# The place of the queries' part in the second half's list of projections

## The chip, the cores and the metric

One core of a Trainium2 chip runs the whole step. The metric is the device time of one execution in microseconds (us). The engines are named as in the profile: PE is the matrix engine (PEld its weight loads), DVE the vector engine, ACT the scalar engine, POOL the GpSimd engine, and SP is the engine whose queue issues nearly all DMAs.

## The reference

One layer is applied to 2048 new frames of a prompt and to 64 frames of a running stream. One projection of the normalised input feeds ten column groups: queries, keys, values and a gate of a differential attention (`qa, ka, va, za`), the same four of a retention branch (`qb, kb, vb, zb`), and two merge gates (`ga, gb`).

```python
h = rmsnorm(x, norm_g) @ w_in
qa, ka, va, za, qb, kb, vb, zb, ga, gb = jnp.split(h, _split_points(), axis=-1)
qa = rmsnorm(qa.reshape(B, T, H_A, 2, DK_A), qn_g)
ka = rmsnorm(ka.reshape(B, T, H_A, 2, DK_A), kn_g)
...
s = jnp.einsum('bqhcd,bkhcd->bhcqk', q, k).astype(jnp.float32) * (DK_A ** -0.5)
s = s - slopes[None, :, None, None, None] * dist[None, None, None]
s = jnp.where(allowed[None, None, None], s, -jnp.inf)
p = jax.nn.softmax(s, axis=-1)
a = p[:, :, 0] - lam * p[:, :, 1]
...
m = ga * (oa @ w_oa) + gb * (ob @ w_ob)
return x + m @ w_out
```

The attention is causal in chunks of 64 frames, so the frames 0 to 1023 need keys and values of the first half alone, and the frames 1024 to 2047 need those of both halves. Everything is float32: every operand of a matrix product is split into a high and a low part of a reduced format, and a product is three matmuls (high by high, high by low, low by high).

## The kernel before, in words

**A planner writes the order out.** The kernel is a set of Python generators, each with a priority. A loop (L197) always advances the most urgent one that may go on by the planner's own clock; a generator yields a time or a condition. The instructions of PE, ACT and DVE stay in the order in which they are written. The clock is an estimate: `P` (L258) adds what a matmul costs on PE, `A`, `V` and `G` what ACT, DVE and POOL take. `take` and `give` (L214, L255) hand out numbered buffers of SBUF and banks of PSUM with the time from which they are free.

**Two streams share PE.** `w_stream` (L2961) makes the projections. Its priority is the lowest (9), so that it fills PE wherever nothing else may run. `z_stream` (L3064, priority 4) makes the attention: first the running stream's, then for each half of the prompt four heads of four pairs of row blocks (`attn_head`, L1845), where `qk_block` makes the scores (L1878, L1879), `softmax` works on ACT and DVE, and `at_pv` transposes (L1990) and multiplies by the values (L1968 to L1970). The attention of a half waits until `w_stream` has set a mark (`kqv00` and `kqv10`, then `kqv01` and `kqv11`): `h_loader`, `q_loader` and `z_stream` look for it, and `head_in` (L1823) adds 9000 ns of the planner's clock. Retention (`ret_stream`, L2436) is a third, more urgent stream; its second part waits for the mark `ret1`.

**The list of the second half.** In L2996 the projections of frames 1024 to 2047 stand as a list. There are two kinds ahead of the last entry:

- A natural part (`natural`, L1230; in the list `wide[0]` values, `wide[1]` keys, `wide[2]` queries, and `later`, the retention's values) makes 512 columns for eight tiles of 128 frames: 192 matmuls, with the frames' tile held and the weights streaming 512 wide. Its weights come as eight pieces of 128 x 512; all eight are kept for all eight tiles, high and low, so 16 buffers are in use. They are given back one piece after the other during the eighth tile.
- A transposed unit (`transposed`, L1426; `plain[0]` to `plain[10]`) makes 256 columns: 144 matmuls in six groups (the first unit has eight groups and 192). Its weights are four pieces, 8 buffers. `plain[2]` and `plain[3]` are the retention's keys.

The last entry, `quad` (L1544), makes the remaining five column pairs in a form with seven products in place of eight; its x-operands come from DRAM through `x_pass` (L1510).

`m0` and `m1` in the list are the marks `kqv0` and `kqv1`; `(None, "nat")` lets `x_again` and `more_rows` go on.

**Weights.** `w_load` (L661) loads the pieces in the order of `self.order`, which is made from the same list (L2998), into three staging buffers `ws`. `next_piece` (L711) takes two buffers, 12 of the kind `w` and 4 of the kind `wx`; ACT writes the high part (L727), POOL the low part (L748).

**After a projection.** A natural tile of queries goes through `fin_qk` (L1289): ACT squares and copies it, DVE sums and scales, PE transposes it (L1340), ACT and DVE split it, and SP stores it to `qT`. A transposed group is copied by ACT (`fin_t`, L1450) and stored.

**The end.** When the attention and the retention are done, `out_prep` (L2561) loads and splits the weights and operands of the output projections; when `quad` is done too, `out_stream` (L2935) follows.

Of the kernel before, what the change touches and what calls it, by code (L numbers as in the profile page):

```python
# [172 lines left out]
class Hybrid:  # L173
# [2787 lines left out]
    def w_stream(self):  # L2961
# [3 lines left out]
        m0, m1 = (None, "kqv0"), (None, "kqv1")  # L2965
# [7 lines left out]
        wide = [(va, lambda half: self.natural(half, self.fin_va(0, 4), False, True), True),  # L2973
                (ka, lambda half: self.natural(half, self.fin_qk("k", 0, 4), False, True), True),
                (qa, lambda half: self.natural(half, self.fin_qk("q", 0, 4), False, True), True)]
        first = [wva, wk, wq, m0, m1]
        seq = []
        early = [(vb, lambda half: self.natural(half, self.fin_vb(), False, True, True), True)]
# [10 lines left out]
        for base, dst, n in ((za, self.zaT, 2), (zb, self.zbT, 2), (ga, self.gaT, 4), (gb, self.gbT, 4)):  # L2989
            for g in range(n):  # L2990
# [2 lines left out]
        later = [(vb, lambda half: self.natural(half, self.fin_vb(), False, True), True)]  # L2993
        plain = [(c0, lambda half, a=a: self.transposed(*a), False) for c0, a in again[:PLAIN]]
        c0s, args = zip(*again[PLAIN:])
        seqs = [first + early + seq, [plain[0], plain[1], wide[0], wide[1], plain[2], wide[2], m0, m1, plain[3],  # L2996
                                      *later, (None, "nat"), (None, "ret"), *plain[4:],
                                      (c0s, lambda half: self.quad(args), "quad")]]  # L2998
        self.order = [[(c[0], c[2] if len(c) > 2 else False) for c in q if c[0] is not None] for q in seqs]
# [203 lines left out]
```

## Time and profile before

| what | value |
|---|---|
| median of 3 runs (lowest to highest) | 1892.78 us (1887.71 to 1893.15) |
| profiled execution, its own time | 1890.56 us |
| span of its trace, first to last instruction | 1888.8 us |
| PE / DVE / ACT / POOL busy | 1869.9 / 1328.1 / 975.9 / 673.6 us |
| second half's projections in the trace | 585.4 to 1531 us |

A row of the table of stretches gives, for a stretch of the span, its length, each engine's busy time in it with the number of its instructions, the clock that PE was granted (1.00 is full), the share of the DMA engines and their rate. A row of the timeline is start, length, engine, line, operation, output and input. A row of the list of waits names the waiting instruction, the one it waited for, the total, the number of times and the longest. Matmuls overlap: one of 512 columns shows about 0.39 us, and the next one starts some 0.23 us after it.

### The profile page before, as it was taken

What the parts mean: (1) busy time and instruction counts of PE and PEld (TensorE: products, weight loads), DVE (VectorE), ACT (ScalarE), POOL (GpSimd) and SP (SyncE); (2) the same over time, 40 slices, a digit from 0 to 9 for tenths busy, and PEclk for the clock granted to TensorE, in tenths of its full rate; (3) what the DMA queues carried; (4) which work ended last, traced back from release to release, by engine and by line L of the source; (5) the groups of instructions that cost most, each with busy time, mean ns of one, the idle gap of its engine ahead of it and who ended that gap; (6) DMA issues with size and microseconds to landing.
All of it is one profiled execution on the core that took longest, in us unless ns stands there. A gap on an engine that the chain in (4) does not pass through costs nothing.

```text
span 1888.8 us, 33022 instructions
## 1 busy us (share of the span) xinstructions
PE 1869.9 (99%) x11090; PEld 1647.0 (87%) x11090; DVE 1328.1 (70%) x3110; ACT 975.9 (52%) x2266; POOL 673.6 (36%) x730
## 2 busy tenths in 40 slices
PE   9999999999999999999999999999999999999999
PEld 7788888888888888899888899999999999998887
DVE  6765757657584776877477676668787868987664
ACT  6434544555434566555455565556676546654221
POOL 2420356555562203031311345342133545522442
PEclk9999999999999999999999999999999999999999
DMA  8664555666857866564622855854633998986452
GB/s 259 210 178 123 167 155 182 180 197 195 248 181 199 216 195 213 154 198 110 177 73 80 206 147 152 211 141 127 184 110 117 270 248 265 272 255 210 166 157 78
DMA packets 402557, 340.09 MB, mean 180 GB/s; under 512 B 85330, under 2 KB 348626, under 8 KB 401363
## 3 DMA queue, kind: packets, MB, share of 16 engines
q1 hardware_dynamic: 402386, 337.97, 61.4%
q8 instruction: 88, 1.44, 0.3%
q14 instruction: 83, 0.67, 0.1%
HBM read 218.27 MB, written 118.75 MB: 178 GB/s over the span
## 4 chain that ended last, share of the span: by engine, by line
PE 84%; DMA 6%; DVE 5%; issue 1%; POOL 1%; ACT 1%; SPq 1%; DVEq 0%; POOLq 0%; ACTq 0%
PE mm L1137 29%; PE mm L989 8%; PE tp L989 4%; PE at L1990 3%; PE s L1878 2%; PE s L1879 2%; PE s L989 2%; PE pv L1970 2%; PE pv L1969 2%; PE pv L1968 2%; PE mm L1564 2%; PE s L2793 1%; PE s L2795 1%; PE s L2794 1%; PE pv L2256 1%
## 5 line engine op out<-in xcount | busy, mean ns | idle before, releaser
L748 POOL TENSOR_TENSOR wl<-ws,wh 128x512 fp32r<-128x512 f32 x109 | 151.7, 1403 | 232.8 <-ACT wh L727 232.1
L1137 PE MATMUL mm<-wh,xh 128*128 128x512 f32 x504 | 203.5, 404 | 0.0
L1137 PE MATMUL mm<-wl,xh 128*128 128x512 f32 x504 | 198.1, 393 | 1.7 <-POOL wl L748 1.7
L1137 PE MATMUL mm<-wh,xl 128*128 128x512 f32 x504 | 198.3, 393 | 0.0
L1137 PE MATMUL mm<-xh,wh 128*128 128x288 f32 (+2 forms) x544 | 179.1, 329 | 0.0
L1137 PE MATMUL mm<-xl,wh 128*128 128x288 f32 (+2 forms) x544 | 176.0, 323 | 0.0
L1137 PE MATMUL mm<-xh,wl 128*128 128x288 f32 (+2 forms) x544 | 175.9, 323 | 0.0
L1918 ACT ACTIVATE row<-row,a_mx 128x1024 f32<-128x1024 f32 (+7 forms) x144 | 149.9, 1043 | 10.2 <-DVE a_mx L1897 10.0
L2006 DVE TENSOR_TENSOR atl<-at,ath 128x512 fp32r<-128x512 f32 (+1 forms) x144 | 92.9, 658 | 82.6 <-ACT ath L2004 82.1
L2004 ACT CAST ath<-at 128x512 fp32r<-128x512 f32 (+1 forms) x144 | 79.2, 564 | 108.9 <-PE at L1990 106.1
L1745 POOL TENSOR_TENSOR r_y<-r_y,r_sq 128x256 f32<-128x256 f32 x32 | 28.7, 896 | 282.1 <-DVE r_sq L1742 220.5
L856 POOL TENSOR_TENSOR wl<-ws,wh 128x256 fp32r<-128x256 f32 x64 | 54.3, 848 | 197.2 <-ACT wh L847 196.9
L1887 DVE CUSTOM_DVE_ANT_0 row<-s,dfar 128x512 f32<-128x512 f32 (+2 forms) x145 | 89.5, 630 | 38.1 <-PE s L1879 37.7
L1137 PEld LDWEIGHTS mm<-wh,xl 128*128 128x128 f32 x504 | 94.7, 188 | 21.5
L1137 PEld LDWEIGHTS mm<-wl,xh 128*128 128x128 f32 x504 | 95.1, 189 | 19.7 <-POOL wl L748 2.5
L1137 PEld LDWEIGHTS mm<-wh,xh 128*128 128x128 f32 x504 | 94.9, 188 | 17.4 <-DVE raw L1308 0.2
L1137 PEld LDWEIGHTS mm<-xh,wl 128*128 128x128 f32 x544 | 102.6, 189 | 6.7
L1137 PEld LDWEIGHTS mm<-xh,wh 128*128 128x128 f32 x544 | 102.6, 189 | 6.5
L1137 PEld LDWEIGHTS mm<-xl,wh 128*128 128x128 f32 x544 | 102.7, 189 | 6.3
L1940 DVE SCALAR_TENSOR_TENSOR row<-row,a_w 128x1024 f32<-128x1024 f32 (+5 forms) x88 | 98.4, 1123 | 0.0
L1878 PE MATMUL s<-K,q 128*128 128x512 f32 (+3 forms) x238 | 91.1, 385 | 0.6 <-DVE a_acc L1887 0.5
L727 ACT CAST wh<-ws 128x512 fp32r<-128x512 f32 x111 | 67.5, 619 | 45.8 <-DMA ws<-wsum 11.2
(543 smaller groups left out, 6070.0 us busy)
## 6 DMA issues: line engine op xcount, KB each, us to landing
ws<-in_w_in_dram SPq DMA_DIRECT2D x155, 256.0 KB, 3.4
q<-qT SPq DMA_DIRECT2D x128, 128.0 KB, 3.4
K<-kT SPq DMA_DIRECT2D x48, 256.0 KB, 4.7
V<-vN SPq DMA_DIRECT2D x24, 512.0 KB, 6.3
row<-in_x_prompt_dram SPq DMA_DIRECT2D x16, 512.0 KB, 4.5
wz<-in_w_in_dram SPq DMA_DIRECT2D x32, 256.0 KB, 4.4
row<-in_cache_k_T_dram SPq DMA_DIRECT2D x32, 256.0 KB, 3.1
row<-in_cache_v_diff_dram SPq DMA_DIRECT2D x32, 256.0 KB, 3.6
```

The costliest lines, as they stand in the source:

```text
L727: self.nc.scalar.copy(h, st)
L748: eng.tensor_sub(l, st, h.bitcast(F32))
L856: nc.gpsimd.tensor_sub(l[:, cs], src, h[:, cs].bitcast(F32))
L989: nc.tensor.matmul(ps, w[:, c], xs[x][c], start=bool(tag) and c == 0 and i == 0, stop=c == 3 and i == 2, skip_group_check=True)
L1137: nc.tensor.matmul(ps, p, q, start=c == 0 and i == 0, stop=c == KC - 1 and i == 2)
L1878: nc.tensor.matmul(ps, q1s, kk, start=True, stop=False)
L1887: nc.vector.tensor_tensor_reduce(out=row[:, k0:k0 + n], in0=ps, in1=tab, scale=-SLOPES[h], scalar=3.0e38, op0=ALU.add, op1=ALU.min, accum_ ...
L1918: nc.scalar.activation(u, u, AF.Exp, bias=mx, scale=-1.0, accum_out=lp[:, k:k + 1])
L1940: nc.vector.scalar_tensor_tensor(out=u0, in0=u1, scalar=w[:, 0:1], in1=u0, op0=ALU.mult, op1=ALU.add)
L1990: nc.tensor.transpose(at[:, w:w + 128], src, self.ident)
L2004: nc.scalar.copy(ah[:, :w], at[:, :w])
L2006: nc.vector.tensor_sub(al[:, :w], at[:, :w], ah[:, :w].bitcast(F32))
```

## The change

In the list of the second half, `wide[2]` (the queries) and `plain[2]` (the first of the two units of retention keys) change places; the two marks stay right behind the queries and so go ahead of `plain[2]` too. No instruction's form changes, and none is added or left out. The order in which the weight pieces are loaded follows, as it is made from the same list.

```diff
         c0s, args = zip(*again[PLAIN:])
-        seqs = [first + early + seq, [plain[0], plain[1], wide[0], wide[1], plain[2], wide[2], m0, m1, plain[3],
+        seqs = [first + early + seq, [plain[0], plain[1], wide[0], wide[1], wide[2], m0, m1, plain[2], plain[3],
                                       *later, (None, "nat"), (None, "ret"), *plain[4:],
                                       (c0s, lambda half: self.quad(args), "quad")]]
```

## The prediction

> **What bounds the kernel now.** I read the page first, then the table of stretches, then PE's list of waits, then single rows of the timelines of PE and POOL.
>
> ```profile
> span 1888.8 us, 33022 instructions
> ...
> PE 1869.9 (99%) x11090; PEld 1647.0 (87%) x11090; DVE 1328.1 (70%) x3110; ACT 975.9 (52%) x2266; POOL 673.6 (36%) x730
> ...
> PE 84%; DMA 6%; DVE 5%; issue 1%; POOL 1%; ACT 1%; SPq 1%; DVEq 0%; POOLq 0%; ACTq 0%
> ```
>
> PE is idle for 1888.8 - 1869.9 = 18.9 us in all, and the chain that ended last runs through it for 84%. A change of order leaves PE the same matmuls; it can win only what PE idles or loses in clock, and it can lose by making PE idle. So the place of the change comes next, cut where the pieces of the list begin and end (all engines, then the projections of line 1137 alone):
>
> ```profile
> core 0: us, PE busy (x) PEld busy (x) DVE busy (x) ACT busy (x) POOL busy (x), PEclk, DMA share, GB/s
> ...
> 738.30:821.40 83.10, 81.44 (x485) 70.58 (x485) 67.65 (x196) 48.93 (x127) 21.07 (x18) 1.00 0.65 187
> 821.40:859.80 38.40, 38.40 (x269) 35.94 (x268) 26.80 (x80) 21.26 (x53) 6.75 (x7) 1.00 0.60 177
> 859.80:922.60 62.80, 62.80 (x348) 53.80 (x347) 41.45 (x107) 34.21 (x82) 11.21 (x10) 1.00 0.49 134
> 922.60:947.30 24.70, 24.70 (x153) 22.61 (x153) 5.11 (x9) 8.67 (x17) 12.86 (x18) 1.00 0.57 170
> 947.30:1037.40 90.10, 89.84 (x496) 77.16 (x495) 69.35 (x202) 48.96 (x98) 11.11 (x8) 1.00 0.25 75
> 1037.40:1388.50 351.10, 350.53 (x2366) 322.84 (x2365) 255.30 (x723) 204.22 (x454) 122.79 (x197) 1.00 0.61 161
> 1388.50:1460.00 71.50, 70.35 (x551) 68.62 (x548) 60.15 (x132) 49.06 (x103) 23.04 (x16) 1.00 0.41 126
> 1460.00:1531.00 71.00, 68.31 (x536) 67.33 (x535) 54.99 (x90) 33.91 (x59) 40.26 (x28) 1.00 0.92 261
> ```
>
> ```profile
> core 0: us, PE busy (x), PEclk, DMA share, GB/s
> ...
> 821.40:859.80 38.40, 26.54 (x144) 1.00 0.60 177
> 859.80:922.60 62.80, 47.16 (x194) 1.00 0.49 134
> 922.60:947.30 24.70, 24.32 (x145) 1.00 0.57 170
> 947.30:1037.40 90.10, 50.26 (x195) 1.00 0.25 75
> ```
>
> The keys run to 821.4, `plain[2]` (144 matmuls) to 859.8, the queries (192) to 922.6, `plain[3]` (144) to 947.3, the retention's values to 1037.4, the seven other transposed units to 1388.5, `quad` to 1531. The reader should see that PE has no idle time from 821.4 to 947.3, although there is next to no attention in the last of these stretches: `plain[3]` is alone there, at 24.3 us.
>
> ```profile
> 873.48 0.39 PE L1879 MATMUL s<-K,q 128*128 128x512 f32 x1
> ...
> 922.65 0.40 PE L1137 MATMUL mm<-xh,wh 128*128 128x512 f32 x1
> ...
> 950.76 0.39 PE L1878 MATMUL s<-K,q 128*128 128x512 f32 x1
> ```
>
> The first half's last scores are at 873.5. The queries end and the mark is set at 922.65. The second half's first scores are at 950.76, 28.1 us behind the mark.
>
> ```profile
> engine line waited for: us in total, times, longest us
> PE at L1564 <- DVE ev L1584: 1.8, 1, 1.8
> PE mm L1137 <- POOL wl L748: 1.7, 2, 1.0
> ...
> PE tp L1719 <- DVE u L1584: 1.1, 1, 1.1
> PE mm L1564 <- DVE ev L1584: 0.8, 2, 0.5
> ```
>
> These are nearly all of PE's waits between 821 and 1531, but for the POOL line, which lies in the stretch before (83.10 - 81.44 = 1.66 us); I need it below.
>
> **The change part by part.**
>
> *The marks come earlier.* Ahead of them PE has one transposed unit less. Alone that is 24.3 us (the row of `plain[3]`), so the mark moves from 922.65 to about 898.3, and the first scores with the same 28.1 us to about 926.4; `plain[2]` then fills the gap as `plain[3]` does now. This saves nothing by itself: PE is full on both sides, and the 24.3 us of `plain[3]` go among the second half's attention, whose stretches (947.3 to 1388.5) are full too, with 0.26 + 0.57 = 0.83 us idle. Worth 0. If that cover failed, up to 24.3 us would lie open; no row suggests it, as `plain[2]` stands ready.
>
> *Queries directly behind keys.* Both are natural parts, and each holds all 16 buffers. Now a unit with 8 buffers lies between them, and the boundaries at 821.4 and 859.8 cost PE nothing. The nearest row is values to keys, the same kind of neighbours:
>
> ```profile
> 731.31 2.54 POOL L748 TENSOR_TENSOR wl<-ws,wh 128x512 fp32r<-128x512 f32 x2 [7.63 <-ACT wh L727]
> ...
> 748.86 1.26 POOL L748 TENSOR_TENSOR wl<-ws,wh 128x512 fp32r<-128x512 f32 x1
> ...
> 810.19 2.52 POOL L748 TENSOR_TENSOR wl<-ws,wh 128x512 fp32r<-128x512 f32 x2 [1.70 <-ACT wh L727]
> ...
> 827.73 1.29 POOL L748 TENSOR_TENSOR wl<-ws,wh 128x512 fp32r<-128x512 f32 x1 [3.14 <-ACT wh L727]
> ```
>
> Eight pieces took from 731.3 to 750.1 there, and PE waited 1.7 us for the last two, though the attention put work between. Around 821 POOL makes eight pieces from 810.2 to 829.0 (four for `plain[2]`, four for the queries); after the change all eight are the queries'. The lower bound is 0: between 821.4 and 859.8 other streams give PE 269 - 144 = 125 matmuls to lay between. The upper bound is the time of refill without any cover. One eighth of the natural part, 47.16 / 8 = 5.9 us, passes while the old tile gives its buffers back and another while the new one takes them: 18.8 - 2 x 5.9 = 7.0 us. I take 1.66, the row of the same neighbours. Behind a wait stand all later matmuls of both streams, as PE keeps its order.
>
> A wait can also cost clock. The rows with the lowest clock in this part of the trace:
>
> ```profile
> core 0: us, PE busy (x) PEld busy (x) DVE busy (x) ACT busy (x) POOL busy (x), PEclk, DMA share, GB/s
> 612.00:614.00 2.00, 1.46 (x12) 1.23 (x10) 0.56 (x1) 1.41 (x4) 2.00 (x2) 1.00 0.67 188
> 614.00:616.00 2.00, 0.81 (x3) 0.67 (x4) 0.00 (x0) 0.00 (x1) 1.41 (x2) 0.89 0.71 209
> 616.00:618.00 2.00, 2.00 (x8) 1.81 (x8) 1.67 (x7) 0.00 (x0) 0.00 (x0) 0.50 0.76 212
> 618.00:620.00 2.00, 2.00 (x14) 1.88 (x13) 0.42 (x4) 0.37 (x1) 0.00 (x0) 0.75 0.88 268
> ...
> 1501.00:1503.00 2.00, 0.23 (x3) 0.03 (x1) 1.76 (x3) 2.00 (x5) 1.19 (x2) 1.00 1.00 263
> ```
>
> After 0.54 + 1.19 = 1.73 us of idle PE the clock lost 2 x (0.11 + 0.50 + 0.25) = 1.72 us; after 1.77 us at 1501 it lost nothing. So a wait of this size costs 0 to 1.7 us more; I take 0, as the two pieces of the row at values to keys, waited for apart, did not lower it. [...]
>
> *Queries beside the first half's attention.* All eight tiles now fall where the last heads work. What their ending costs is bounded by the stretch that holds all eight now: at most 41.45 / 8 = 5.2 us of DVE and 34.21 / 8 = 4.3 us of ACT for each, the attention's own work counted in. In 821.4 to 859.8 there are 38.40 - 26.80 = 11.6 us free on DVE and 17.1 on ACT. Some four tiles fall there, so DVE is late by 4 x 5.2 - 11.6 = 9.2 us at the very most, and then the first half's last pairs are late, while PE has the queries and `plain[2]`. Worth 0 with that cover, up to 9.2 without it.
>
> *What stands behind `plain[3]` comes later.* In 947.3 to 1037.4 the projections have 50.26 of 90.10 us, 56%. At that rate `plain[3]`, now among the attention, takes 24.3 / 0.56 = 43 us from 922.6, and the retention's values end at 922.6 + 43 + 90 = 1056, 19 us later. The marks for `x_again` and the second part of the retention move with them.
>
> ```profile
> L1466 POOL TENSOR_TENSOR xa<-xh,xl x80: 375/394/1584, 932.6 to 1284.1; 128x96 f32<-128x96 f32 x48, 128x128 f32<-128x128 f32 x32
> ```
>
> The last of `x_again`'s sums starts at 1284.1, 104 us ahead of `quad`, which needs them; 19 us leave 85. Worth 0, and if all of the margin went, each us later would cost one.
>
> *The other boundaries.* Queries to a transposed unit has no idle time at 922.6, nor has a unit to the retention's values at 947.3 beyond 0.26 us; two units in a row occur all through 1037.4 to 1388.5, with 0.57 us idle. SP's queue gets the eight loads of the queries ahead of four of `plain[2]`; the same loads pass through it, and PE's list shows no wait on a weight load. Worth 0.
>
> *Attention ends earlier.* It runs with priority, so its end moves from about 1460 to about 1436, and `quad`, whose end is set by PE's sum, stays alone for some 95 us in place of 71. Preparing the output then starts 24 us earlier and falls less on `quad`'s last products, where PE waits for DVE (1.8 + 0.8 us). Bounds: a loss of 0.9 us if the idle time of the last stretch (71.00 - 68.31 = 2.69) grew with its length (2.69 x 24 / 71), a gain of 2.6 if both waits went. DVE is busy for 54.99 of 71 there and the same work remains, so I take half the gain, 1.3.
>
> Sum: +1.66 - 1.3 = +0.4 us on 1890.56 us of the profiled execution (span and 1.8 us around it), 1890.9. That execution lies 2.2 us under the median of the runs; I give the forecast on the median's scale: 1892.78 + 0.4 = 1893.2.
>
> **The rivals.**
>
> *Slower: the refill is not covered.* Place: the queries' first tile, about 821 to 832. It decides if the planner lays less than some 7 us of other work into that tile. Then PE waits the 7.0 us, and the clock takes 1.7 more: 1892.8 + 8.7 = 1901.5. For it: at values to keys PE waited although there was cover, because ACT's high part came late and the planner had not reckoned with it. Against it: the 125 matmuls of others that lie there now.
>
> *Faster: the late waits go.* If the earlier end of the attention takes `quad`'s waits and the first ones of the output stage with it:
>
> ```profile
> PE s L2669 <- DVE ga L2682: 1.7, 1, 1.7
> PE s L2670 <- DVE ogl L2626: 1.1, 1, 1.1
> PE at L2670 <- DVE ogl L2626: 0.6, 2, 0.4
> ```
>
> That is 1.8 + 0.8 + 1.1 + 1.7 + 1.1 + 0.6 = 7.1 us, and without a wait at the boundary 1885.7. Against it: the output stage's operands are bounded by a few buffers, so an earlier start does not store them up.
>
> *It does not do what it says.* The second half's attention could still begin at about 950, if its loads and not the mark set the time: the 28.1 us were then no lag behind the mark. PE is filled meanwhile by `plain[2]` and `plain[3]`, and only the boundary is paid: 1892.8 + 1.7 = 1894.5.
>
> **How the numbers follow.** Forecast 0.42, not doing what it says 0.08, refill uncovered (or its like, a stall behind a late buffer) 0.33, late waits gone 0.17. A measurement of this kernel can tell about 0.3%, 5.7 us: the first two cases are no change (1893.2 and 1894.5), the third is slower, the fourth faster. The forecast's own range is 1890 (both waits of `quad` gone, none at the boundary: 1892.8 - 2.6) to 1897 (1892.8 + 1.7 + 1.7 of clock + 0.9). For 8 in 10 the range must reach most of the third case and half of the fourth: 1886.5 to 1905, the upper end half an uncovered refill (3.5) above 1901.5.
>
> **What would show it.** In the changed kernel's trace the natural rows of line 1137 run without a gap from 656 to about 898; the first second-half scores stand at about 926, the last transposes of the attention at about 1436, and `quad` ends at 1531. PE's list of waits should have about 1.7 us more under line 748. Wrong would be: PE idle for more than 4 us between 815 and 930, a clock under 1.00 there, the start of the second half's scores after 940, or `quad` ending more than 6 us from 1531.

## The result and the profile after

| what | before | after |
|---|---|---|
| median in one comparison, 20 runs each (lowest to highest) | 1891.03 us (1887.71 to 1894.80) | 1894.67 us (1890.93 to 1899.35) |
| ratio, with its 95% interval | | 1.0019 [1.0013, 1.0025] |
| profiled execution, its own time | 1890.56 us | 1891.76 us |
| span of its trace | 1888.8 us | 1890.0 us |

The kernel is slower by 0.19%, about 3.6 us, and the interval leaves out 1. The loss lies under the 0.3% taken as no change, and the time within 1.5 us of the time forecast. The profiled execution lies 2.9 us under the median of its kernel, so the trace shows only a part of the 3.6 us. The places of things say more than its sums. One execution in the experiments below, of `rms_late`, ran in a slow state (2190.87 us at a clock of 0.785) and is left out of ratios and means.

The table of stretches after the change for all engines, cut where the pieces of the list and of the attention begin and end:

```profile
core 0: us, PE busy (x) PEld busy (x) DVE busy (x) ACT busy (x) POOL busy (x), PEclk, DMA share, GB/s
...
821.40:874.50 53.10, 53.10 (x266) 44.15 (x265) 33.97 (x96) 23.47 (x60) 7.70 (x6) 1.00 0.49 142
874.50:898.30 23.80, 23.52 (x149) 21.26 (x148) 7.50 (x19) 11.26 (x24) 12.50 (x18) 1.00 0.65 188
898.30:922.60 24.30, 23.66 (x162) 21.65 (x161) 20.42 (x51) 16.48 (x37) 8.10 (x7) 1.00 0.58 163
922.60:953.20 30.60, 30.60 (x218) 28.89 (x217) 19.02 (x58) 16.38 (x39) 2.72 (x3) 1.00 0.40 105
953.20:1050.20 97.00, 97.00 (x563) 84.94 (x562) 76.80 (x226) 58.04 (x116) 16.39 (x13) 1.00 0.38 106
```

And the projections of line 1137 alone in the first of these stretches (length, PE busy, clock, DMA share, GB/s):

```profile
821.40:874.50 53.10, 46.97 (x193) 1.00 0.49 142
```

Three things are to be seen. PE has no idle time at all from 821.4 to 874.5, so keys to queries costs nothing. The queries end, and the mark is set, at 874.5: that is 48 us earlier than before (922.6), not 24. And they fill 46.97 of those 53.10 us, where the queries before had 47.16 of 62.80: other work has been pushed out of their stretch.

What was pushed out is the attention of the first half. From PE's timeline of the changed kernel, the last scores of the first half, the first scores of the second half, and the last transposes of the attention:

```profile
918.96 0.39 PE L1878 MATMUL s<-K,q 128*128 128x512 f32 x1
...
936.57 0.39 PE L1878 MATMUL s<-K,q 128*128 128x512 f32 x1
...
1455.38 0.38 PE L2015 MATMUL pv<-ident,a_e 128*1 128x128 f32 x2
```

The first half's last scores moved from 873.5 to 919, 46 us later. The second half's first scores moved from 950.8 to 936.6, 14 us earlier. The end of the attention stands where it stood; the same row before the change:

```profile
1455.16 0.38 PE L2015 MATMUL pv<-ident,a_e 128*1 128x128 f32 x2
```

Why it was pushed out is in the rows of one bank of PSUM, `tp`, between 818 and 905 (a row: line, engine, output and input, number, shortest/median/longest ns, first and last start). Before:

```profile
L1340 PE MATMUL tp<-ident,raw x24: 270/272/273, 824.9 to 898.6; 128*128 128x128 f32 x24
L2369 PE MATMUL tp<-row x24: 271/275/276, 836.2 to 872.4; 128*128 128x128 f32 x24
L1719 PE MATMUL tp<-r_hi,ones x5: 279/279/364, 842.4 to 903.0; 128*128 128x256 f32 x5
```

After:

```profile
L1340 PE MATMUL tp<-ident,raw x44: 270/272/273, 824.5 to 885.9; 128*128 128x128 f32 x44
L2369 PE MATMUL tp<-row x16: 270/275/275, 893.0 to 898.4; 128*128 128x128 f32 x16
L1719 PE MATMUL tp<-r_hi,ones x2: 279/321/363, 890.0 to 901.8; 128*128 128x256 f32 x2
```

Three kinds of work take this one bank here: the transposes that end a tile of keys or queries (line 1340, in `fin_qk`), the sums of the attention's normalisation (line 1719) and the retention's transposes (2369). Before, they took turns. After, line 1340 issues all of its transposes by 885.9, and 1719 and 2369 get the bank only from 890.0 and 893.0 on. The last 1719 ahead of this gap is at 810.66, so no sum is made for 79 us. Not all of that is waiting for the bank. A sum can start when DVE has made its second operand (line 1714); after the change that was here, for the sum at 890.0 (rows of PE and of DVE):

```profile
810.66 0.37 PE L1719 MATMUL tp<-r_hi,ones 128*128 128x256 f32 x1
...
832.15 0.43 DVE L1714 TENSOR_TENSOR r_lo<-r_sq,r_hi 128x256 fp32r<-128x256 f32 x1
```

The same operand and its sum before:

```profile
832.75 0.43 DVE L1714 TENSOR_TENSOR r_lo<-r_sq,r_hi 128x256 fp32r<-128x256 f32 x1
...
842.36 0.28 PE L1719 MATMUL tp<-r_hi,ones 128*128 128x256 f32 x1
```

A sum that was ready at 832.6 got the bank 57 us later; before, it was ready at 833.2 and got it 9 us later. The cause is in the order of the requests in `fin_qk`:

```python
            yield from self.take("tp")
            ...
                    nc.tensor.transpose(tp[:, ...], raw[:, c:c + 128], self.ident[:r, :r])
            ...
            yield from self.take("thi")
            yield from self.take("tlo")
```

An ending takes `tp`, transposes, and then waits for `thi` with the bank still in its hands. Of `thi` there is one buffer, and it comes free when, by the planner's clock, the store that reads it has landed. The instructions on this buffer, from 824 to 890 in the changed kernel:

```profile
L1350 ACT ACTIVATE thi<-tp,gq x8: 672/702/706, 845.8 to 887.8; 128x512 fp32r<-128x512 f32 x8
L285 SPq DMA_DIRECT2D qT<-thi x8: 359/376/482, 846.5 to 889.6; - x8
...
L1355 ACT CAST thi<-tp x3: 585/586/588, 825.2 to 837.8; 128x512 fp32r<-128x512 f32 x3
...
DMA to landing us min/median/max: 2.3/2.3/6.0
```

Three uses by keys and eight by queries follow each other from 825.2 to 887.8. Endings have priority 0 and the sums of line 1719 priority 1, so in the planner's order the next ending is served each time the bank comes free. Before the change `plain[2]` lay between the two rows of endings, and the attention got the bank in that pause.

PE shows next to none of this as idle time, since the queries and `plain[2]` fill it. The waits that remain lie late. PE's list of waits from 656 to 1540 (engine, line, waited for: us in total, times, longest):

```profile
PE mm L1137 <- POOL wl L748: 2.3, 2, 1.4
PE mm L1564 <- DVE u L1584: 1.8, 2, 1.5
PE at L1564 <- DVE ev L1584: 1.1, 2, 0.6
PE s L1564 <- DVE ev L1584: 1.1, 2, 0.7
PE mm L1564 <- DVE ev L1584: 1.1, 2, 0.6
```

The two waits on line 748 lie at 749.8 (values to keys, as before) and at 1112. The others are `quad`'s. From `quad`'s first matmul to its last, and from there to the end, before:

```profile
1388.50:1531.00 142.50, 138.67 (x1085) 135.95 (x1083) 115.14 (x221) 82.97 (x162) 63.30 (x44) 1.00 0.66 193
1531.00:1888.80 357.80, 350.55 (x2238) 317.61 (x2236) 257.55 (x408) 151.96 (x352) 141.49 (x106) 1.00 0.66 204
```

After:

```profile
1398.50:1533.20 134.70, 129.50 (x1016) 127.02 (x1016) 106.49 (x185) 75.49 (x147) 64.88 (x45) 1.00 0.72 208
1533.20:1890.00 356.80, 351.14 (x2241) 319.03 (x2239) 255.64 (x405) 150.76 (x350) 138.64 (x105) 0.99 0.67 203
```

PE idles 142.50 - 138.67 = 3.8 us in `quad` before and 5.2 us after; the output stage idles 7.3 and 5.7 us. The clock of 0.99 in the last row is one lowered stretch, seen between 1544 and 1552, behind a wait of 1.9 us:

```profile
PE s L2669 <- DVE ga L2682: 1.9, 1, 1.9
```

```profile
1544.00:1552.00 8.00, 6.15 (x38) 5.93 (x38) 5.32 (x12) 5.27 (x15) 3.09 (x4) 0.79 0.86 262
```

It lost 8 x 0.21 = 1.7 us. The trace before lost as much at 614 to 620, so these two executions do not differ by the clock. Every run lists its span and its mean granted clock, so the runs can be split, as an estimate since the clock is given to three places, into span x (1 - clock), lost to the clock, and span x clock, the rest. The means (with the error of the mean): before, 1.5 ± 0.2 and 1887.2 ± 0.3 us over the 31 runs that stand beside `again` below (those of the table list no clock); after, 3.6 ± 0.5 and 1888.9 ± 0.3 us over the 20 runs of the table; `again`, the same kernel in the same comparison as the 31, 2.2 ± 0.7 and 1888.7 ± 0.5 us over 11 runs. So the rest is longer by 1.5 to 1.7 us in both, and the clock takes 2.1 us more in one and 0.8 in the other. The split is rough: one run of `banks` lists a clock of 0.946, while its span of 1895.2 us is like its neighbours'.

### The profile page after: what moved, and what is told of

Same layout as the page of the kernel before. It is cut to its first block, busy times and chain, and to the rows that moved or that the text cites. A ratio compares the mean times of both kernels' runs of the same rounds, so it can differ in the third digit from the quotient of the medians.

```text
span 1890.0 us, 33039 instructions
## 1 busy us (share of the span) xinstructions
PE 1868.9 (99%) x11090; PEld 1646.3 (87%) x11090; DVE 1336.0 (71%) x3110; ACT 976.4 (52%) x2266; POOL 675.0 (36%) x730
## 4 chain that ended last, share of the span: by engine, by line
PE 47%; DMA 3%; DVE 1%; SPq 1%; POOL 1%; issue 1%; ACT 0%; DVEq 0%; POOLq 0%; ACTq 0%
PE mm L1137 12%; PE at L1990 2%; PE mm L1564 2%; PE s L1879 2%; PE s L1878 2%; PE pv L1970 1%; PE pv L1969 1%; PE pv L1968 1%; PE s L2795 1%; PE s L2794 1%; PE s L2793 1%; PE s L2669 1%; PE at L2669 1%; PE s L2670 1%; PE at L2795 1%; PE mm L2794 1%
## 5 line engine op out<-in xcount | busy, mean ns | idle before, releaser
L1878 PE MATMUL s<-K,q 128*128 128x512 f32 (+3 forms) x236 | 89.3, 380 | 0.0
L1879 PE MATMUL s<-K,q 128*128 128x512 f32 (+3 forms) x236 | 86.0, 366 | 0.9 <-DMA q<-qT 0.9
```

Of the source, the lines that this page charges most:

```text
L1878: nc.tensor.matmul(ps, q1s, kk, start=True, stop=False)
L1879: nc.tensor.matmul(ps, q2s, kk, start=False, stop=True)
```

## The experiments

Three theories stood at the start. Theory A has the loss come from the blocked bank, which keeps the attention's end at 1455. Theory B puts it in `quad`'s own waits, for its banks of PSUM or for DVE, wherever the attention ends. Theory C puts it in the weights of two natural parts behind each other. In short edits, `plain` and `wide` are as in the list.

**again.** The changed kernel as it is, beside the others.

> The changed kernel as it is. In its first trace the second half's scores begin at 936.6 us, the first half's last scores are at 919 (873 before), the attention ends at 1455 as before, and PE waits 4.9 us between 1398 and 1533 for DVE under line 1584 (2.6 us before, and 1.1 for the same line at 1438). Theory A (bank tp: the queries' ending follows the keys' without a break, holds the one bank tp, and the first half's last pairs and the retention stand behind it), theory B (the late DVE waits in quad) and theory C (weights of two natural parts behind each other) all expect 1.0019 of the kernel before, within 0.001, and the same places again.

Measured: 1892.48 us, ratio 1.0011 [1.0002, 1.0020]. The places repeat: first half's last scores 920.7, second half's first 938.3, attention's end 1457.1. `quad` runs from 1400.3 to 1540.0, with other waits than in the first trace (1398 to 1560):

```profile
PE s L1564 <- DVE ev L1584: 4.8, 4, 2.1
PE mm L1564 <- DVE u L1584: 1.8, 2, 1.5
PE at L1564 <- DVE ev L1584: 1.0, 1, 1.0
```

```profile
1490.00:1510.00 20.00, 16.29 (x104) 15.27 (x103) 19.31 (x32) 12.33 (x22) 13.46 (x9) 0.83 0.93 281
```

The clock lost 20 x 0.17 = 3.4 us there. The same instructions in the same order gave 5.2 us of idle PE in `quad` in one execution and 7.7 in the other. So one trace of each kernel does not tell a few us apart at this place; means over runs must.

**rms_first.** The endings let the attention's sums go first at the bank.

```diff
+            yield lambda: self.rmsw == 0 or self.ap is self.first
             yield from self.take("tp")      # fin_qk
...
+        self.rmsw += 1
         yield from self.take("tp")          # rms_t
+        self.rmsw -= 1
```

> The changed list, and the transposes of the queries' and keys' endings (line 1335) stand back from bank tp while a root-mean-square of the attention (line 1717) waits for it. Theory A: the first half's last scores come back to about 875, the second half's first scores come to about 900, the attention ends near 1430, and the ratio to the kernel before falls to 1.000 or under it (0.998 to 1.000). Theory B: unless the late waits go, 1.002; if the attention's earlier end takes the waits in quad away, 0.999. Theory C: 1.002, as the weights are the same.

Measured: 1892.26 us, ratio 1.0006 [0.9997, 1.0015]. The sums (now line 1722) are back among the endings:

```profile
L1341 PE MATMUL tp<-ident,raw x44: 270/272/273, 824.2 to 895.6; 128*128 128x128 f32 x44
...
L1722 PE MATMUL tp<-r_hi,ones x4: 276/279/364, 842.2 to 898.2; 128*128 128x256 f32 x4
```

The first half's last scores, the second half's first:

```profile
907.62 0.39 PE L1882 MATMUL s<-K,q 128*128 128x512 f32 x1
...
919.21 0.48 PE L1881 MATMUL tp<-K,q 128*128 128x512 f32 x1
```

Theory A had looked for 875, for 900 and for a ratio of at most 1.000. Both places are missed, and the ratio of 1.0006 lies above, though its interval reaches down to 0.9997. The last scores come 13 us earlier than in `again` (920.9), but still 34 us later than before the change. Sums now start at 842.2, 862.8 and 883.2, where before the change they started at 842.4, 850.9, 862.7 and 875.1. What else holds the first half back is not shown. The end of the attention moved to where the prediction had looked for it, or further:

```profile
1425.97 0.38 PE L2018 MATMUL pv<-ident,a_e 128*1 128x128 f32 x2
```

Put into the kernel before, the edit leaves every instruction where it was. So it changes nothing but who gets the bank first, and what follows from that in the planner's order, and this moves the first half's last scores and the attention's end. The time came down by some 0.05 to 0.13%, less than the intervals can separate from the changed kernel.

**rms_late and rms_late2.** The same, with the marks behind `plain[2]`, so that the second half's attention may start as late as with the blocked bank but without the block. One kernel, measured twice, on two chips.

```diff
-... wide[1], wide[2], m0, m1, plain[2], plain[3],
+... wide[1], wide[2], plain[2], m0, m1, plain[3],
```

> As rms_first, and the two marks stand behind the third transposed unit, so that the second half's attention begins some 24 us later, near where it does in the kernel before (930 to 950). What is left of the change is then the order of the weights and endings alone. Theory A: 1.000 (0.999 to 1.001), between the kernel before and rms_first. Theory B: as the waits in quad show, 1.000 with 2 to 3 us of them and 1.002 with 5. Theory C: 1.002.

> The kernel of rms_late once more, for a trace and a second measurement; its first gave 0.9994 of the kernel before. Theory A (bank tp): 0.999 to 1.0005, the first half's last scores near 890 and the second half's first ones near 930 to 950, and fewer waits of PE between 1398 and 1540 than the changed kernel's 4.9 us. Theory C (weights): 1.002.

Measured: 1888.95 us, 0.9994 [0.9985, 1.0003], and 1890.16 us, 0.9997 [0.9988, 1.0005]. That is the kernel before's time within the interval, both times below the changed kernel's. The weights come in the changed kernel's order, and theory C's 1.002 lies outside both intervals. The places, from the trace of the second measurement:

```profile
942.01 0.39 PE L1881 MATMUL s<-K,q 128*128 128x512 f32 x1
...
1435.58 0.38 PE L2018 MATMUL pv<-ident,a_e 128*1 128x128 f32 x2
```

```profile
1408.50:1536.50 128.00, 119.61 (x926) 117.30 (x926) 93.07 (x144) 65.51 (x127) 66.67 (x46) 0.99 0.79 228
1536.50:1889.60 353.10, 349.32 (x2242) 317.77 (x2240) 253.25 (x404) 149.86 (x348) 136.47 (x103) 1.00 0.65 202
```

The second half's scores begin later than after the change (942 against 937), and yet the attention ends 20 us earlier. The end is therefore not set by the beginning alone. `quad` then idles 8.4 us, 4.6 more than before, and the output stage 3.8, 3.5 fewer: in this execution the waiting moves from one stage to the other and the sum, 12.2 against 11.1 us, is nearly kept. Theory A had the ratio and the second half's first scores right, but the first half's last scores stand at 909.4 in place of 890, and PE waits 8.3 us from 1398 to 1560, more than the changed kernel's 4.9.

Over all runs the split says more than the one trace. The rest is 1884.1 ± 0.5 and 1884.7 ± 0.5 us, against 1887.2 and 1887.1 of the kernel before beside them; lost to the clock are 3.0 ± 0.4 and 3.6 ± 0.5 us, against 1.5 and 1.4. By it this order saves 2.4 to 3.1 us of waiting, and the clock takes 1.6 to 2.2 of them back. Why its clock is lower is not shown.

**banks.** `quad` may take two more banks of PSUM, in the changed kernel.

```diff
-... (("tp",) if self.wo is None else ("s", "at"))
+... (("tp",) if self.wo is None else ("s", "at", "pv", "tp"))
```

> The changed kernel, and quad may use the banks pv and tp beside mm, s and at once the attention has ended. Theory B: the waits for DVE under line 1584 in quad (3.3 us of them behind 1498) fall under 1 us and the ratio to the kernel before comes to 1.000 (0.9990 to 1.0008). Theories A and C: the time moves by less than what these waits are worth, as PE's lost time comes back as waits of the output stage, 1.0012 to 1.0020.

Measured: 1894.59 us, 1.0020 [1.0010, 1.0030]. The waits for `ev`, DVE's emptying of a bank, fell from 3.3 to 1.1 us in all, and waits for the split x-operand stand in their place (1390 to 1560):

```profile
PE tp L1564 <- DVE xl L1529: 4.0, 2, 2.7
PE pv L1564 <- DVE xl L1529: 2.3, 1, 2.3
```

These are waits for DVE, as the others were. Theory B's 1.000 is missed, and 1.0020 is the upper end of what A and C had said. The number of banks is not the limit; DVE is late, and PE meets it at one tile or at the next.

**wo_dve, late_wo_dve and wo_pool.** If DVE is late, where the output weights' low parts are made should matter. `quad`'s last 60 us share DVE and POOL with them. Two kernels with opposite edits in the changed kernel; `late_wo_dve` is one more run of the same kernel as `wo_dve`.

```diff
-... self.split_fin("oz", ..., (kp + q) % 3 == 0, slot, q), 2)
+... self.split_fin("oz", ..., False, slot, q), 2)     # wo_dve: all on DVE
+... self.split_fin("oz", ..., True, slot, q), 2)      # wo_pool: all on POOL
```

> The changed kernel, with the low parts of the output weights (line 2477) all on DVE, 16 in place of 10, and none on POOL. Theory B1 (quad's late waits are DVE's own work): about 6 x 0.7 to 1.1 = 4 to 7 us more DVE work in the last 60 us of quad, more waits under line 1584, ratio to the kernel before 1.002 to 1.004. Theory B2 (DVE is late there because POOL's instructions hold its operations with two SBUF operands: 0.68 us alone, 1.4 to 1.9 beside POOL): POOL works 6 x 1.4 = 8 us less, DVE's mean under line 2477 falls from about 1.0 towards 0.8 and the ratio is 1.000 to 1.0015. Theory A: no change from 1.0015.

> A second look at the kernel of wo_dve for a further trace: the clock of PE falls to half after some waits of PE of 1.5 us and more in quad's last stretch and not after others, and differs from execution to execution. All theories: within 0.3% of the kernel before.

> The changed kernel, with the low parts of the output weights all on POOL, 16 in place of 6. Theory B1: DVE loses 10 us of work in quad's last stretch, the waits under line 1584 go, and the ratio falls to 0.999 to 1.0005. Theory B2: POOL's 13 us more lengthen DVE's other operations there (line 1529 above 1.4 us), the waits stay, 1.0015 to 1.003. Theory A: 1.0015.

Measured: 1892.01 us, 1.0006 [0.9998, 1.0015], a single 1893.82 us, and 1890.76 us, 1.0005 [0.9997, 1.0014]. Opposite edits gave the same ratio, so the split between the two engines is not shown to be the cause: B1 missed with `wo_dve`, B2 with `wo_pool`. Of B2's places one came (without POOL's six, DVE's mean under line 2477 fell from 1.01 to 0.87 us) and one did not (with POOL's 16, DVE's mean under line 1529 was 1.22 us, not above 1.4; 1.33 in the changed kernel). In the single run PE waited 2.0, 1.9 and 1.2 us among others from 1398 to 1560, and its mean clock of 0.999 puts 1.9 us on the clock in the whole execution, about as much as one lowered stretch of the traces above cost (1.7 us); in `again` the clock fell to 0.66 from 1500 to 1510, where PE idled 2.25 us.

**unit_between.** Another way to a pause between the two rows of endings: `plain[1]` goes between keys and queries, and the queries keep their place ahead of `plain[2]`.

```diff
-... plain[0], plain[1], wide[0], wide[1], wide[2], m0, m1, plain[2], plain[3],
+... plain[0], wide[0], wide[1], plain[1], wide[2], m0, m1, plain[2], plain[3],
```

> The list alone, no other edit: the second transposed unit moves from ahead of the values to between keys and queries, and the marks stand, as in the changed kernel, ahead of the third and fourth unit. The queries' marks come as early as in the changed kernel, but the endings of keys and queries no longer follow each other. Theory A (bank tp): the first half's last scores stay near 875, no gap of 50 us or more in them, and the ratio to the kernel before is 0.999 to 1.0005. Theory D (the early mark and the longer mixing with the attention cost by themselves): 1.001 to 1.002.

Measured: 1899.15 us over 5 runs, 1.0046 [1.0032, 1.0059]. A miss. The gap of 65 us in the first half's scores is gone, as the theory of the bank has it, but the last ones stand at 906.6 and not near 875. The list's start moved too: the values now begin 38 us earlier, and PE waits at places ahead of `quad` where the changed kernel shows no wait (656 to 1560):

```profile
PE tp L1878 <- DMA q<-qT: 1.6, 1, 1.6
PE s L1878 <- DVE a_acc L1887: 1.4, 1, 1.4
```

Two things were changed at once, so it says only that an order can cost half a per cent.

**late_pool, first_pool and before_pool.** `wo_pool`'s edit in `rms_late`, in `rms_first` and in the kernel before.

> rms_late with the low parts of the output weights all on POOL, as in wo_pool. If the two effects add: 0.9996 less 0.001, so 0.9980 to 0.9992, below the kernel before. If the output stage takes back what quad no longer waits for: 0.9993 to 1.0000, as rms_late.

> rms_first with the low parts of the output weights all on POOL. If the effects add: 0.9990 to 1.0000. If not: 1.0003 to 1.0010, as rms_first.

> The kernel before with the low parts of the output weights all on POOL. If this edit is worth the same in any order: 0.999 (0.9982 to 0.9996). If it is worth something in the changed order alone, where the end of quad and the output's preparation meet in another way: 0.9995 to 1.0005.

Measured: 1889.23 us, 0.9998 [0.9989, 1.0007]; 1893.31 us, 1.0018 [1.0009, 1.0026]; 1889.86 us, 0.9997 [0.9988, 1.0006]. The parts do not add up: the same edit is worth nothing that can be measured in two of them and, if anything, a loss in the third (1.0018 against the 1.0006 of `rms_first`, with intervals that overlap; 1.0018 lies outside both of its expectations). There the stretches' table has this row:

```profile
1480.00:1490.00 10.00, 5.48 (x29) 4.77 (x28) 10.00 (x14) 8.18 (x14) 9.46 (x6) 0.73 1.02 289
```

DVE is busy through all ten us of it and PE for about half, at a clock of 0.73. By the split of the runs `first_pool` loses 6.2 us to the clock, against 2.0 of the kernel before in that comparison, and its rest is 1 us shorter. No version is shown to be faster than the kernel before: the best, `rms_late`, has 1 in its interval.

## Why the prediction was right, and where its steps were not

The verdict was right: the loss is smaller than the 0.3% that the prediction took as the least it could tell. That the time lies only 1.5 us from the forecast is luck. Forecast was +0.4 us, measured +3.6, and the kernel before came out 1.8 us under the median of three runs on which the forecast stood; of the sum's two terms, +1.66 and -1.3, neither came. None of the stated signs of being wrong showed in the first trace (second half's scores from 936.6, `quad`'s end at 1533.2; in `again` `quad` ends at 1540, 9 us off), so they were too weak to find the step that failed.

- *PE stays full from 821 to 947 and the marks' move is worth nothing by itself*: right, with no idle time in 821.4 to 874.5 and 0.9 us in 874.5 to 953.2 (0.28 + 0.64).
- *Queries directly behind keys, 1.66 us under line 748, bounds 0 to 7.0*: the mechanism was considered rightly and the term was too large. PE waited 0 us there; the 0.6 us more under line 748 lie at 1112. With it falls the rival of the uncovered refill, to which 0.33 was given.
- *Queries beside the first half's attention, worth 0 with DVE late by at most 9.2 us*: this is the step that failed. It counted the busy time of DVE and ACT and did not ask who holds what. The endings of keys and queries ran on without a pause and held the one bank `tp`, and a sum of the attention that was ready waited 57 us for it, 48 more than before. The first half's last scores came 46 us later, not at most 9; letting the sums go first takes back 13 of these (`rms_first` against `again`), and what makes the others is open. That this cost PE nothing at the place is right.
- *The mark at 898, the first scores at 926*: the mark came at 874.5, because the attention no longer lay among the queries, and the scores at 936.6, because the first half's end, not the mark, set their start: with the marks behind `plain[2]`, and nothing else changed, the planner writes the same instructions in the same order.
- *What stands behind `plain[3]` comes 19 us later*: near. The retention's values ended at 1050, 13 us later, and the last of `x_again`'s sums started at 1287.6 in place of 1284.1, well ahead of `quad`.
- *The attention ends at 1436, `quad` stays alone for 95 us and gains 1.3 us*: it ended at 1455, and `quad` idled 1.4 us more than before in the profiled execution and 3.8 us more in `again`. Where the bank was freed (`rms_late2`) the attention did end at 1435.6 and the output stage did become 4.7 us shorter, as the step argued, but `quad`'s own waits rose by as much. Over all runs of that kernel the split shows 2.4 to 3.1 us less waiting, in the direction of the step, and a clock that takes most of it back.
- *Clock, taken at 0, bounds 0 to 1.7*: too small, and looked for at the wrong place. Nothing was lost at 821; the split of the runs puts 2.1 us on the clock for the changed kernel, and 0.8 us in `again`, with errors of 0.6 and 0.7. Later than the place of the edit, the lowered stretches of the changed kernel's two traces stand at waits for DVE, at `quad`'s end (`again`) and at the first output tiles.
- *The rival in which the second half's attention still begins at about 950*: by its time and by the attention's end the result lies nearer to this one (chance 0.08, 1894.5 us) than to the forecast, while the second half's first scores (936.6) stand between the two (926 and 950). The cause is the late end of the first half, where the loads were suspected.

Shown: who gets the bank first moves the first half's last scores by 13 us and the attention's end by 31 us (`rms_first` against `again`). Not shown: what makes the other 34 us of the first half's delay. Likely, not shown: that the bank is a reason of the 3.6 us. The kernels with the bank freed and the marks late are at the level of before, 0.0014 and 0.0025 under the changed kernel's two ratios at the nearest and the farthest; but freeing the bank alone (`rms_first`, 1.0006) is not clear of the changed kernel, `wo_pool` with the bank blocked comes to 1.0005, and `first_pool` with it freed to 1.0018. Open: how much of the loss is the blocked bank, how much the clock, and how much the chance by which DVE's work and `quad`'s tiles meet in its last 60 us.

## What to carry to other kernels

When two stages are brought next to each other, list the single buffers and banks that both take, and what each still waits for while it holds one; busy time on the engines does not show a bank that is held across a store. In a kernel whose matrix engine is full, a new order moves waits rather than work, so look for them at the next stage with little cover, however far behind the edit. Before a difference of a few us is explained from two traces, take a second trace of the same kernel and compare the granted clock of all runs.

## What the runs showed of the hardware

**Lowered clock behind short waits.** In the traces of the two kernels the clock fell to half for about 3.4 us, from 615.5 to 618.9 before the change (0.51 in that stretch) and from 1547.4 to 1550.8 after it (0.50), and each time that cost 1.7 us. The first stood behind two waits of 1.5 and 0.3 us close together, the second behind one of 1.9 us. `again` (0.66 from 1500 to 1510) and `banks` (0.67 from 1518 to 1524, 0.76 from there to 1530) each lost 3.4 us at one place, twice as much. PE's idle time there went from 1.6 us (610 to 620 in `unit_between`, at a clock of 0.92) to 4.0 us (1.06 + 2.91 from 1510 to 1524 in `banks`). Behind other waits of that size the clock did not fall: in the kernel before it was 1.00 from 1500 to 1512, behind a wait of 1.8 us that ended at 1503. By their mean clocks the profiled executions lost from next to nothing (1.000 in `late_pool`) to some 7.6 us (0.996 in `unit_between`). What decides between two waits of one length was not found.

**DVE beside POOL.** DVE's subtractions of two operands in SBUF ran slower where POOL was already at work on SBUF, 1.66 us against 0.68. From the timelines of DVE and of POOL in the changed kernel:

```profile
1496.95 0.68 DVE L2477 TENSOR_TENSOR w_o_diffl<-wst,w_o_diffh 128x512 fp32r<-128x512 f32 x1
1497.55 0.71 DVE L1529 TENSOR_TENSOR xl<-xraw,xh 128x544 fp32r<-128x544 f32 x1
...
1503.56 1.66 DVE L2477 TENSOR_TENSOR w_o_retl<-wst,w_o_reth 128x512 fp32r<-128x512 f32 x1
```

```profile
1497.69 1.70 POOL L748 TENSOR_TENSOR wl<-ws,wh 128x512 fp32r<-128x512 f32 x1 [1.60 <-ACT wh L727]
...
1503.39 1.29 POOL L2473 TENSOR_TENSOR w_o_diffl<-wst,w_o_diffh 128x512 fp32r<-128x512 f32 x1 [0.99 <-ACT w_o_diffh L2470]
1504.63 1.72 POOL L748 TENSOR_TENSOR wl<-ws,wh 128x512 fp32r<-128x512 f32 x1
```

The same form took 0.68 us alone and 1.66 us with POOL's two beside it, and POOL's second one 1.72 us where the first took 1.29. Where DVE began first, at 1497.55, it took 0.71 us, and POOL's operation that began 0.14 us later took 1.70. By these rows, moving the low parts from DVE to POOL does not simply free DVE, which fits with `wo_dve` and `wo_pool` coming out alike (1.0006 and 1.0005).
